# Two-layer hybrid backbone on one core: seams of layer 0 reordered, the even class's sums a step earlier, odd classes' stores on another queue

## The chip, the cores and the metric

One Trainium2 chip, one of its cores. The metric is the device time of one execution in microseconds; lower is better. The core has five engines with a queue of their own each: TensorE (PE, matmuls), VectorE (DVE), ScalarE (ACT), GpSimd (POOL) and SyncE (SP). Each runs its own instructions in order and waits on semaphores for the others'. Transfers are issued here by SP (`ld`) and by POOL (`ldr`), now and then by ACT (`lda`), and stand in the issuing engine's order.

## The reference

Two layers over 1024 latent tokens and 256 context tokens of width 1024, all float32. Cut to what matters here:

```python
def swiglu(u, w_gate, w_up, w_down):
    return (jax.nn.silu(u @ w_gate) * (u @ w_up)) @ w_down
def long_conv(u, filt, skip):
    uf = jnp.fft.rfft(u, n=2 * L, axis=1)
    ff = jnp.fft.rfft(filt, n=2 * L, axis=0)
    return jnp.fft.irfft(uf * ff[None], n=2 * L, axis=1)[:, :L] + u * skip
def hyena_mix(p, ...):
    x1, x2, v = jnp.split(short_conv(p, conv_w, conv_b), 3, axis=-1)
    filt = hyena_filters(L, w1, b1, freq, w2, b2, w3)
    v = x1 * long_conv(v, filt[:, 0], skip[0])
    return x2 * long_conv(v, filt[:, 1], skip[1])
def mixer_ab(u, ...):                       # layer 0
    p = u @ w_in
    return jnp.concatenate([fourier_mix(p[..., :512]), hyena_mix(p[..., 512:], ...)], axis=-1) @ w_out
# layer 1: neighbourhood attention, 16 heads, bias rpb by relative position; latents also see the context
for i in range(2):
    sh1, sc1, g1, sh2, sc2, g2 = split(silu(cond) @ ada_w[i] + ada_b[i], 6)   # cond: c or c_ctx
    h = h + g1 * mixer(rms_norm(h) * (1 + sc1) + sh1)
    h = h + g2 * swiglu(rms_norm(h) * (1 + sc2) + sh2, ...)
return rms_norm(h_lat, final_g)
```

The context tokens go through the same steps in layer 0; they have no output of their own in layer 1.

## The kernel before

Matmuls that need float32 accuracy take operands as a high and a low part: `split` casts the high part on ScalarE (`last_hi`, L350) and subtracts it on VectorE for the low part (`last_lo`, L352). Weights arrive in `ws` tiles (four buffers) and are split into `wh` and `wl` (two buffers each), so a pair can be split only when the pair two before it has been used. The other tiles come from pools with fixed counts: `s` (21 of 1024 columns, `S4`; 35 of 512, `S2`), `g` (4, `G`), `t` (6, `T`), `tk` (4, `TK`), and PSUM banks `ps` (6) and `pq` (2). A tile's name in the views is its pool's, without numbers.

The program is recorded from Python generators that yield after each step, so that stages can be woven: `next(g)` records one more step of a side stage. A scheduler then sets the order on each engine by a timeline of its own; `follow(x)` tells it to put what is recorded inside behind instruction x. After that each engine's order is fixed.

The stages by time in the profile: start and filter MLP to 56 us; the input projection (`in_proj`), woven with the long filters' taps (`filter_raw`) and spectra (`spectrum_l`, once per filter: about 145 to 207 and 262 to 317 us) and with the context's filters, to 430 us; the long convolutions forward and back to 635 us (`inverse_last` ends them); the output projection (`out_proj`) to 751.7 us; layer 0's FFN (`ffn`, then `down`) to about 1560 us; values, attention (about 1590 to 2190 us), its output projection and layer 1's FFN to the end.

The places that the change touches:

- `spectrum_l` multiplies a filter's taps with cosine and sine matrices (`ff_l`, loaded by POOL into `tk` tiles) in four classes, in the order 2, 3, 0, 1, each in two halves p with two operands k. Classes 0 and 2 are even, 1 and 3 odd. `operands()` makes an operand from sums of taps (`sums` for even classes, L958 to L970), and splits it; `ready` holds operands that are made ahead. TensorE's banks are copied out by ScalarE (L1043), the odd classes' by VectorE sums (L1051, L1053), and stored.
- `filter_raw` multiplies taps by windows `in_win_l` that SP loads; VectorE reads the banks at L822.
- `late_groups` loads the conditioning (`load_cond`), takes its silu (L556) and makes the last adaLN group by VectorE sums (L584). It is woven with `inverse_last` and `out_proj`.
- `out_proj` calls `after1` when a part of the columns is done. `rms_begin` adds up squares (`square`: ScalarE L609, VectorE L614) over the partitions by matmuls with a column of ones; `rms_end` spreads the result by two more.
- `ffn` first does the context's columns, 22 blocks of gate and up, with `second` (the norm of latent columns, `wino_second`) woven in.
- `down` ends in a loop of 22 blocks over the context's columns (L2230); `hook` weaves `after2` in: the norm of layer 1 for the columns done (`norm_block`: VectorE L656, ScalarE L658, VectorE L659).
- `attn_item` scores two chunks of one head; its position bias is loaded into two `g` tiles (c0 = 0) or a `bias` tile. The first 48 items are "cross": they use a `tk` tile for a transpose by DMA. The 16 items after them don't.

## Time and profile before

| | |
|---|---|
| runs | 2848.94 us median of 3 (2848.43 to 2850.37) |
| profiled execution | 2850.3 us, its span 2848.5 us |
| busy in the span | PE 97%, PEld (weight loads of TensorE) 81%, DVE 72%, ACT 46%, POOL 19% |
| DMA | 554.20 MB, mean 195 GB/s |
| granted TensorE clock | 0.99 of full speed, mean |

A row of the timeline gives start, duration, engine, line, operation, tile written <- tiles read, shape and count; in brackets stands how long the engine was idle before it, and what ended that. "PE ps L346 <- ACT s L1043: 3.6, 2, 3.2" reads: matmuls of line 346 waited 3.6 us in all, two times, at most 3.2 us, until ScalarE's L1043 was done. PEclk is the granted clock of TensorE as a share of full speed.

### The profile page before, as it was taken

How to read it: one execution, taken by the hardware profiler on the slowest of the kernel's cores; microseconds unless marked ns; L12 is line 12 of the kernel's file. 1: busy time of each engine (PE TensorE's matmuls, PEld its weight loads, DVE VectorE, ACT ScalarE, POOL GpSimd, SP SyncE). 2: the span in 40 equal slices, each digit the busy share in tenths (PEclk: the TensorE clock that was granted, in tenths of full speed). 3: DMA queues.
4: the chain of work that ended last, by engine and by line, in shares of the span. 5: the costliest groups of instructions: out<-in, count | busy, mean ns of one | idle time of the engine just before them, and what ended most of it. 6: DMA issues, size and time to landing. Idle time of an engine off the chain costs nothing. (4 is left out here: it accounts for less than half of the span.)

```text
span 2848.5 us, 43624 instructions
## 1 busy us (share of the span) xinstructions
PE 2762.6 (97%) x15610; PEld 2314.2 (81%) x15610; DVE 2044.6 (72%) x3531; ACT 1319.0 (46%) x2269; POOL 543.9 (19%) x880
## 2 busy tenths in 40 slices
PE   7999999999999999999999999999999999999998
PEld 4876778788898888888879888888887788888887
DVE  6767577867877888876777437778768977664556
ACT  5433336443554333333455337788755533333434
POOL 2210235331001221222020002333211122112000
PEclk9999999999999999999999999999999999999999
DMA  7356535665666656658884436877855366434763
GB/s 268 121 182 219 155 93 186 215 211 189 214 196 200 211 196 210 213 202 323 306 305 152 133 115 152 201 197 197 243 191 207 133 239 229 140 106 170 234 195 133
DMA packets 296886, 554.20 MB, mean 195 GB/s; under 512 B 81872, under 2 KB 128658, under 8 KB 296670
## 3 DMA queue, kind: packets, MB, share of 16 engines
q1 hardware_dynamic: 227966, 352.67, 39.4%
q0 software_dynamic: 61504, 185.65, 18.6%
q10 hardware_dynamic: 7200, 13.11, 1.4%
q8 instruction: 123, 2.02, 0.3%
q14 instruction: 93, 0.76, 0.1%
HBM read 405.01 MB, written 118.76 MB: 184 GB/s over the span
## 5 line engine op out<-in xcount | busy, mean ns | idle before, releaser
L1932 PE MATMUL ps<-s,s 128*128 128x512 f32 x2012 | 497.6, 391 | 3.5 <-DVE s L1823 1.9
L1932 PEld LDWEIGHTS ps<-s,s 128*128 128x128 f32 x2012 | 378.3, 188 | 84.0 <-DVE s L1823 3.2
L346 PE MATMUL ps<-s,wh 128*128 128x256 f32 (+1 forms) x1776 | 401.9, 331 | 10.8 <-ACT s L1043 3.2
L346 PEld LDWEIGHTS ps<-s,wh 128*128 128x128 f32 x1776 | 295.2, 190 | 46.4 <-ACT s L350 4.1
L346 PE MATMUL ps<-s,wl 128*128 128x256 f32 (+1 forms) x888 | 267.4, 329 | 1.7 <-DVE wl L352 1.6
L2109 PE MATMUL ps<-s,s 128*128 128x512 f32 (+1 forms) x1000 | 259.9, 383 | 3.3 <-DVE s L352 3.2
L350 ACT CAST s<-s 128x1024 fp32r<-128x1024 f32 (+2 forms) x192 | 172.6, 927 | 193.1 <-DMA s<-d 177.3
L346 PE MATMUL pq<-s,wh 128*128 128x512 f32 (+1 forms) x848 | 260.8, 389 | 0.4 <-ACT wh L350 0.3
L352 DVE TENSOR_TENSOR wl<-ws,wh 128x1024 fp32r<-128x1024 f32 (+1 forms) x141 | 168.3, 1195 | 119.8 <-ACT wh L350 114.2
L350 ACT CAST wh<-ws 128x1024 fp32r<-128x1024 f32 (+1 forms) x141 | 144.7, 1026 | 204.9 <-PE ps L346 85.0
L352 DVE TENSOR_TENSOR s<-s,s 128x1024 fp32r<-128x1024 f32 (+2 forms) x170 | 190.9, 1154 | 59.4 <-ACT s L350 59.1
L346 PE MATMUL ps<-s,s 128*128 128x65 f16 (+4 forms) x2736 | 226.2, 235 | 7.3 <-DVE st L2446 2.6
L350 ACT CAST s<-t 128x512 fp32r<-128x512 f32 (+2 forms) x238 | 133.9, 581 | 195.8 <-PE ps L1932 69.2
L2109 PEld LDWEIGHTS ps<-s,s 128*128 128x128 f32 x1000 | 184.5, 188 | 41.3 <-DVE s L352 5.0
L352 DVE TENSOR_TENSOR s<-t,s 128x512 fp32r<-128x512 f32 (+2 forms) x238 | 151.2, 651 | 72.6 <-ACT s L350 59.6
L1932 PE MATMUL ps<-s,wh 128*128 128x512 f32 x624 | 194.9, 390 | 0.0
L346 PEld LDWEIGHTS ps<-s,wl 128*128 128x128 f32 x888 | 165.6, 190 | 18.4 <-DVE wl L352 2.5
L337 POOL DMA_DIRECT2D d<-s x186 | 101.0, 544 | 375.5 <-DVE s L1739 92.5
L346 PEld LDWEIGHTS pq<-s,wh 128*128 128x128 f32 x848 | 151.1, 190 | 22.1 <-ACT wh L350 0.7
L346 PE MATMUL pq<-s,wl 128*128 128x512 f32 (+1 forms) x424 | 162.0, 382 | 0.6 <-DVE wl L352 0.6
L2109 PE MATMUL ps<-s 128*128 128x512 f32 (+1 forms) x500 | 150.9, 385 | 0.0
L346 PEld LDWEIGHTS ps<-s,s 128*128 128x128 f32 (+1 forms) x816 | 126.6, 192 | 21.8 <-ACT t L2448 2.7
(486 smaller groups left out, 5465.0 us busy)
## 6 DMA issues: line engine op xcount, KB each, us to landing
s<-d SPq DMA_DIRECT2D x282, 256.0 KB, 3.9
d<-s POOLq DMA_DIRECT2D x170, 256.0 KB, 3.7
s<-in_down SPq DMA_DIRECT2D x150, 256.0 KB, 4.2
s<-in_ada_w POOLq DMA_DIRECT2D x64, 512.0 KB, 4.9
ws<-in_up SPq DMA_DIRECT2D x44, 512.0 KB, 3.7
d<-g POOLq DMA_DIRECT2D x86, 256.0 KB, 3.0
ws<-in_gate SPq DMA_DIRECT2D x42, 512.0 KB, 4.8
d<-tk POOLq DMA_DIRECT2D x66, 256.0 KB, 4.0
```

The lines of the kernel that those rows point to most:

```text
L337: self.last_ldr = self.nc.gpsimd.dma_start(out, in_).ins
L346: self.last_mm = self.nc.tensor.matmul(o, l, r, start=st, stop=sp).ins
L350: self.last_hi = nc.scalar.copy(hi, src).ins
L352: self.last_lo = eng.tensor_tensor(lo, src, hi.bitcast(F32), SUB).ins
L1932: nc.tensor.matmul(ps, x[:, sl], y, start=first and j == 0 and x is wh and y is xh, stop=j == 3 and x is wl, skip_group_check=True)
L2109: m = nc.tensor.matmul(acc[j][:, c0:c1], x[:, sl], y[:, xs], start=first and k == 0, stop=last and k == 2, skip_group_check=True)
```

## The change

Five groups of edits, all in the order of work and in where tiles and transfers go. No matmul is added or taken away; two activation table loads are added.

1. `spectrum_l`: class 0's f0 and its first sums are made during class 3's second half, behind that half's operands, all in `s2` tiles; operands are made three ahead instead of four; the odd classes' 16 stores go by POOL instead of SP.
2. `late_groups`: the silus are recorded three steps later, behind the inverse's last high cast.
3. `ffn` for layer 0: the first gate block's weights are loaded and split during the output projection (`early`), and the norm's `rms_begin` and `rms_end` of columns 512 to 1023 are steps of `second`, behind the first and the second block, not ahead of the FFN; `second` starts at the first block instead of the third.
4. `after2` for the columns 512 to 1023: one norm block per step instead of two, each behind the low part made two norm blocks earlier.
5. `attn_item`: the bias of items that are not cross, with hd = 0 and c0 = 0, goes to `tk` tiles.

```diff
@@ late_groups
-        self.load_cond(wide=where == "s4")
+        self.load_cond(wide=where == "s4", act=False)
+        yield
+        yield
+        yield
+        with self.follow(self.inv_hi):
+            for t in self.cond:
+                for x in t:
+                    self.nc.scalar.activation(x, x, AF.Silu)
@@ spectrum_l, sums
-            t, u, x = self.T(), self.S2() if i else self.T(), self.T() if i else self.S2()
+            t, u, x = (self.T(), self.S2(), self.T()) if i else (self.S2(), self.S2(), self.S2())
@@ spectrum_l, operands
+            even0 = []
             for i in classes:
-                if i == 0:
-                    f0 = self.f0 = self.S2()
...
-                even = []
+                even = even0 if i == 0 else []
...
-                            if p == 0:
+                            if p == 0 and i:
                                 even.append(sums(i, k))
...
                         yield xh, xl, mt[k]
+                        if i == 3 and p:
+                            if k == 0:
+                                f0 = self.f0 = self.S2()
...
+                            even0.append(sums(0, k))
 
         ops = operands()
-        ready = [next(ops) for _ in range(4)]
+        ready = [next(ops) for _ in range(3)]
@@ spectrum_l, odd classes
-                        self.ld(self.frg[("l", o, 1, f)][eo], x)
+                        self.ldr(self.frg[("l", o, 1, f)][eo], x)
...
-                        self.ld(d[eo], t)
+                        self.ldr(d[eo], t)
@@ inverse_last
+        self.inv_hi = self.last_hi
@@ ffn
-                gh, gl = self.weights(a["gate"][l, fb], wide=wide)
+                gh, gl = early.pop() if fb == 0 else self.weights(a["gate"][l, fb], wide=wide)
...
-                if fb >= 2:
-                    with self.follow(last):
-                        next(second, None)
+                with self.follow(last):
+                    next(second, None)
@@ attn_item
-            bias = [self.G(F32, 384), self.G(F32, 384)]
+            new = self.G if cross or hd else self.TK
+            bias = [new(F32, 384), new(F32, 384)]
@@ run
             else:
                 drain(first)
-                rest.append(self.rms((1,))[0])
 
         def first_row():
-            yield from self.wino_first(h, 0, 3, rest.pop())
+            for k, _ in enumerate(self.wino_first(h, 0, 3, rest.pop())):
+                if k == 6:
+                    self.p3 = 1
+                    early.append(self.weights(a["gate"][0, 0], wide=3))
+                yield
@@ run, after2
+            los = []
             for b in range(KB):
...
-                self.norm_block({b: h3.ap(0, b, pc)}, b, pc, 1, 0, u1, r)
-                if b % 2:
+                with self.follow(los.pop() if los and pc == 1 else None):
+                    self.norm_block({b: h3.ap(0, b, pc)}, b, pc, 1, 0, u1, r)
+                los.append(self.last_lo)
+                if b % 2 or pc == 1:
                     yield
@@ run
-        self.ffn(0, uf, h3, hs0, (x for r in rest for x in self.wino_second(h, 0, 3, r)), after2, hd)
+        def second():
+            with self.follow(self.last_mm):
+                c = self.rms_begin(1)
+            yield
+            with self.follow(self.last_mm):
+                r = self.rms_end(1, c)
+            yield
+            yield from self.wino_second(h, 0, 3, r)
+
+        self.ffn(0, uf, h3, hs0, second(), after2, hd, early=early)
```

In the changed kernel later lines have higher numbers (L1043 becomes L1053, L656 and L659 become L663 and L666).

What it does to the order, at three places. ScalarE in the second filter's spectrum, from the copies of class 2 to those of class 3 (`s` <- `t` are casts of operands), before:

```order
L1043 COPY s_669_2474<-ps_2443 128x512
L1043 COPY s_672_2478<-ps_2444 128x512
L962 CAST s_681_2505<-t_2501 1x512
L350 CAST s_683_2512<-t_2500 128x512
L350 CAST s_688_2529<-t_2523 128x512
L1043 COPY s_692_2540<-ps_2490 128x512
L1043 COPY s_695_2543<-ps_2491 128x512
L1068 ACTIVATE s_698_2575<-ps_2278,c_287 128x256
```

And after:

```order
L1053 COPY s_666_2468<-ps_2437 128x512
L1053 COPY s_669_2472<-ps_2438 128x512
L969 CAST s_676_2495<-s_674_2491 1x512
L350 CAST s_679_2504<-t_2502 128x512
L350 CAST s_686_2525<-s_673_2490 128x512
L1053 COPY s_690_2536<-ps_2484 128x512
L1053 COPY s_693_2539<-ps_2485 128x512
L1078 ACTIVATE s_696_2571<-ps_2278,c_287 128x256
```

Two casts stand between the one-row cast and the copies in both, but they are of other operands: before, of class 0's first two (t_2500 and t_2523, the results of L965 and L970); after, of class 3's last and class 0's first. Class 0's second has moved behind the copies.

VectorE at the end of layer 0, from two low parts of down weights (`wl`) into the norm of columns 512 to 1023, before:

```order
L352 TENSOR_TENSOR wl_14519<-ws_14517,wh_14518 128x1024
L656 SCALAR_TENSOR_TENSOR t_14583<-s_3020_12687,c_99,t_14505 128x512
L656 SCALAR_TENSOR_TENSOR t_14587<-s_3021_12689,c_99,t_14505 128x512
L656 SCALAR_TENSOR_TENSOR t_14630<-s_3022_12691,c_99,t_14505 128x512
L656 SCALAR_TENSOR_TENSOR t_14634<-s_3023_12693,c_99,t_14505 128x512
L656 SCALAR_TENSOR_TENSOR t_14674<-s_3078_12968,c_99,t_14505 128x512
L659 SCALAR_TENSOR_TENSOR s_3328_14581<-t_14583,c_99,s_3328_14581 128x512
L352 TENSOR_TENSOR wl_14553<-ws_14551,wh_14552 128x1024
```

And after:

```order
L352 TENSOR_TENSOR wl_14519<-ws_14517,wh_14518 128x1024
L663 SCALAR_TENSOR_TENSOR t_14583<-s_3020_12687,c_99,t_14505 128x512
L666 SCALAR_TENSOR_TENSOR s_3328_14581<-t_14583,c_99,s_3328_14581 128x512
L352 TENSOR_TENSOR wl_14553<-ws_14551,wh_14552 128x1024
L663 SCALAR_TENSOR_TENSOR t_14624<-s_3021_12689,c_99,t_14505 128x512
L352 TENSOR_TENSOR wl_14596<-ws_14594,wh_14595 128x1024
L663 SCALAR_TENSOR_TENSOR t_14664<-s_3022_12691,c_99,t_14505 128x512
L666 SCALAR_TENSOR_TENSOR s_3329_14582<-t_14624,c_99,s_3329_14582 128x512
L666 SCALAR_TENSOR_TENSOR s_3341_14662<-t_14664,c_99,s_3341_14662 128x512
L352 TENSOR_TENSOR wl_14634<-s_3338_14632,wh_14633 128x1024
```

Between low parts stand two, one and three instructions of the norm, where the first gap held six.

SP in the attention, where the last bias tiles of pair 7 are loaded (s <- d are reloads of attention outputs for the output projection), before:

```order
L331 DMA s_4631_22056<-d_15886 128x512
L331 DMA s_4641_22126<-d_15887 128x512
L331 DMA g_22037<-in_bias 128x384
L331 DMA s_4642_22128<-d_15888 128x512
L331 DMA g_22038<-in_bias 128x384
L331 DMA bias_22343<-in_bias 128x2x384
L331 DMA g_22237<-in_bias 128x384
```

And after:

```order
L331 DMA tk_22037<-in_bias 128x384
L331 DMA t_21520<-d_15137 32x4x128 x4
L331 DMA tk_22038<-in_bias 128x384
L331 DMA bias_21948<-in_bias 128x2x384
L331 DMA bias_22131<-in_bias 128x2x384
L331 DMA s_4584_21804<-d_15877 128x512
L331 DMA t_21690<-d_15137 128x2x128
```

The two loads 22037 and 22038 stood behind the reloads and now stand ahead of the first of them (s_4584).

More of the change, by code (lines that the diff above doesn't have):

```diff
@@ L978, in operands @@
         def operands():
+            even0 = []
             for i in classes:
-                if i == 0:
-                    f0 = self.f0 = self.S2()
-                    V.tensor_copy(f0, fe)
-                    V.tensor_tensor(f0[0:1, :], fe[0:1, :], fo[0:1, :], ADD)
-                    V.scalar_tensor_tensor(f0[0:1, :], f0[0:1, :], 0.5, self.taps0[o][0:1, :], op0=MUL, op1=ADD)
-                even = []
+                even = even0 if i == 0 else []
                 for p in (0, 1):
@@ L1005, in operands @@
                         yield xh, xl, mt[k]
+                        if i == 3 and p:
+                            if k == 0:
+                                f0 = self.f0 = self.S2()
+                                V.tensor_copy(f0, fe)
+                                V.tensor_tensor(f0[0:1, :], fe[0:1, :], fo[0:1, :], ADD)
+                                V.scalar_tensor_tensor(f0[0:1, :], f0[0:1, :], 0.5, self.taps0[o][0:1, :], op0=MUL, op1=ADD)
+                            even0.append(sums(0, k))
         ops = operands()
-        ready = [next(ops) for _ in range(4)]
+        ready = [next(ops) for _ in range(3)]
         yield
@@ L1975, in wino_begin, with ffn @@
         return s
-    def ffn(self, l, u, h, hs, second, after, keep=None, begun={}):
+    def ffn(self, l, u, h, hs, second, after, keep=None, begun={}, early=()):
         nc, a = self.nc, self.a
@@ L2002, in ffn @@
         if u is not None:
+            last = None
             for fb in range(NFB):
                 wide = 3 if fb < NFB - 2 else 2
-                gh, gl = self.weights(a["gate"][l, fb], wide=wide)
+                gh, gl = early.pop() if fb == 0 else self.weights(a["gate"][l, fb], wide=wide)
                 uh, ul = self.weights(a["up"][l, fb], wide=wide)
@@ L2652, in spill @@
                     self.ldr(hs[b][:, pc * 512:pc * 512 + WID[pc]], h.ap(0, b, pc))
-        rest = []
+        rest, early = [], []
         def after1(pcs):
```

## The prediction

> **What bounds the kernel now.** I read the page's busy line first, then the waits of TensorE by cause, then stretches of one clock window each, then the order of events around every wait that lies where the diff works.
>
> ```profile
> span 2848.5 us, 43624 instructions
> PE 2762.6 (97%) x15610; PEld 2314.2 (81%) x15610; DVE 2044.6 (72%) x3531; ACT 1319.0 (46%) x2269; POOL 543.9 (19%) x880
> ```
>
> TensorE is busy for all but 2848.5 - 2762.6 = 85.9 us, and the diff adds or removes no matmul. It can win only idle time of TensorE, and the time in which TensorE runs at half clock. The waits by cause (us in total, times, longest):
>
> ```profile
> engine line waited for: us in total, times, longest us
> ...
> PE pq L346 <- DVE s L822: 3.7, 3, 1.7
> PE ps L346 <- ACT s L1043: 3.6, 2, 3.2
> ...
> PE ps L2230 <- DVE wl L352: 3.0, 2, 2.1
> PE ps L346 <- DVE st L2446: 2.6, 1, 2.6
> ...
> PE pq L346 <- DVE tk L614: 2.3, 1, 2.3
> ...
> PE ps L346 <- DVE wl L352: 1.6, 1, 1.6
> ```
>
> The longest of each of these six lies at a place that the diff touches. A wait costs more than itself where the clock falls. In stretches of 3.4 us (busy columns PE to POOL, then the granted clock, DMA share, GB/s):
>
> ```profile
> core 0: us, PE busy (x) PEld busy (x) DVE busy (x) ACT busy (x) POOL busy (x), PEclk, DMA share, GB/s
> ...
> 281.80:285.20 3.40, 0.24 (x2) 0.24 (x3) 3.27 (x6) 1.39 (x3) 0.00 (x0) 0.99 0.57 139
> 285.20:288.60 3.40, 3.40 (x18) 3.40 (x17) 2.67 (x5) 3.40 (x7) 0.00 (x0) 0.50 0.11 39
> ...
> 755.90:759.30 3.40, 3.40 (x19) 3.40 (x18) 2.23 (x4) 2.61 (x6) 0.00 (x0) 0.54 0.82 251
> 1534.10:1537.50 3.40, 1.61 (x15) 1.42 (x13) 3.40 (x5) 2.49 (x3) 0.00 (x0) 1.00 0.35 131
> 1537.50:1540.90 3.40, 3.09 (x14) 3.09 (x15) 3.40 (x6) 0.72 (x1) 0.00 (x0) 0.55 0.44 146
> ...
> 2070.00:2073.40 3.40, 3.02 (x33) 2.75 (x33) 2.18 (x7) 3.04 (x8) 0.00 (x0) 0.55 0.44 160
> ...
> 666.60:670.00 3.40, 2.80 (x14) 2.05 (x12) 3.40 (x12) 0.79 (x2) 0.87 (x2) 1.00 0.19 77
> 670.00:673.40 3.40, 2.37 (x14) 2.11 (x15) 3.40 (x9) 0.14 (x1) 0.55 (x2) 1.00 0.45 122
> ```
>
> After the waits of 3.21, 2.29, 2.10 and 2.57 us one stretch runs at about half clock: 3.4 us of work at half speed is 1.7 us lost. The 1.63 us at 669.4, split over two stretches (0.60 and 1.03 idle), costs no clock. So a stretch with some 1.8 us idle costs 1.7 us more, and where a smaller wait falls on the grid is luck.
>
> **The change part by part.** Terms are against the profiled execution (2850.3 us; its span is 2848.5).
>
> *Spectrum of the second long filter.* ScalarE casts operands in order, and its copies that empty TensorE's banks (L1043) stand among them:
>
> ```profile
> 279.54 0.62 ACT L350 CAST s<-t 128x512 fp32r<-128x512 f32 x1 [2.50 <-DVE t L965]
> 283.81 0.62 ACT L350 CAST s<-t 128x512 fp32r<-128x512 f32 x1 [3.65 <-DVE t L970]
> 284.33 1.06 ACT L1043 COPY s<-ps 128x512 f32<-128x512 f32 x2
> ...
> 284.96 0.64 PE L346 MATMUL ps<-s,wh 128*128 128x256 f32 x2 [3.21 <-ACT s L1043]
> ```
>
> Before, the cast at 283.81 waits for VectorE's L970 ahead of the two copies. With operands three ahead that cast stands behind them: the casts that remain in front need nothing later than L965's result, for which the row at 279.54 waited, so the copies end by about 281.2, before TensorE needs them at 281.75. The 3.21 us go, and the 1.7 of clock. What is late next: the last operand of class 3 now has its low part on VectorE behind the first sums, about 0.35 us too late. And the loads that GpSimd issues for class 1 get their buffers some 2.3 us before use:
>
> ```profile
> L337 POOL DMA_DIRECT2D tk<-in_ff_l x12: 527/528/597, 263.3 to 305.7; - x12
> ...
> DMA to landing us min/median/max: 2.5/4.4/7.0
> ```
>
> 4.4 - 2.3 = 2.1 us of wait, where today 1.0 us is lost (0.67 at 306.75, 0.34 at 309.08): +1.1, with ends 0 (landing in 2.5) and +3.7 (in 7.0). Waits: -3.2 + 0.35 + 1.1 = -1.8; clock -1.7. The even class's sums now lie in the s2 tiles instead of t; they are the same VectorE instructions, their f0 copy and first sums only pass behind one operand, so nothing is added to VectorE. The first filter's spectrum has the same reordering but waits under 1 us in all: 0, with ends -1.0 and +0.6.
>
> *Odd classes' stores by GpSimd.* SP loses 16 issues, POOL gains 16 of 0.53 us, 8.4 us on an engine that is busy 19%: nothing, while the loads behind them on POOL have slack, some 2 us for the tightest pair. On SP they stood ahead of the window loads:
>
> ```profile
> 211.51 0.69 DVE L822 TENSOR_TENSOR s<-pq,s 128x512 f32<-128x512 f32 x1 [3.02 <-DMA s<-in_win_l]
> ...
> 189.71 16.73 SPq L331 DMA_DIRECT2D d<-s  x7
> 206.49 0.99 SPq L331 DMA_DIRECT2D s<-in_win_l  x2
> ```
>
> SP was held 16.7 us until the odd class's sums existed. Without them the windows land before 208.5 and L822 starts 3 us sooner; TensorE's first wait for it, 1.67 us at 210.6, goes. But the next matmuls need a weight load whose buffer TensorE frees, and its landing sets their start, so most of the 1.3 and 1.4 us after it only merge to a longer wait that may cost clock. Between -1.7 (the first wait) and +1.0 I take -0.5.
>
> *Output projection's first weights.* VectorE has ten adaLN reductions (L584) between two low parts of weights, so the second comes late:
>
> ```profile
> 660.30:669.70 9.40, 6.91 (x19) 1.00 0.34 126
> ...
> 653.50 0.69 DVE L352 TENSOR_TENSOR s<-t,s 128x512 fp32r<-128x512 f32 x1 [3.98 <-ACT s L350]
> ```
>
> 6.9 of 9.4 us are L584 alone, and all of it is late because VectorE had waited 3.98 us for a cast that stood behind ScalarE's silus (L556), which wait for their loads. With the silus moved behind the inverse's last hi cast, four reductions pass ahead of the first low part and eight stay between: 2 x 0.67 less, and the inverse's low parts are done up to 4 us sooner. The 1.63 us go: -1.6, ends 0 and -1.9. The adaLN sums themselves are wanted some 40 us later, so their delay is hidden.
>
> *Seam to the FFN.* Before, the projection's last block is followed by a wait for the squares' sum and the eight column matmuls:
>
> ```profile
> 754.01 1.05 PE L346 MATMUL pq<-c,tk 128*128 128x1 f32 x8 [2.29 <-DVE tk L614]
> ...
> 760.89 1.28 ACT L2011 ACT_TABLE_LOAD   x1
> ```
>
> After, the first gate block, whose weights are split during the projection, runs in that wait. By the durations in these rows the new order goes: the first up block's low part ends 0.8 us late; rms_begin follows it, rms_end the next pair. The fourth gate block waits for its high part, which ScalarE has behind two casts that need VectorE's L1846 and L1853 after the row scale: 1.9 us. Two more table loads (1.28 us each) fall on ScalarE while TensorE works on blocks of 2.7 us, and are in these waits. So 2.29 becomes 2.7: +0.4; the clock's 1.7 is saved, as neither new wait fills a stretch by itself. Ends: -2.3 (no new wait) and +0.4.
>
> *End of layer 0.* VectorE does five and then seven of the norm's instructions ahead of low parts of weights that have only two buffers:
>
> ```profile
> 1527.45 3.40 DVE L656 SCALAR_TENSOR_TENSOR t<-s,c,t 128x512 f32<-128x512 f32 x5
> ...
> 1531.42 1.22 DVE L352 TENSOR_TENSOR wl<-ws,wh 128x1024 fp32r<-128x1024 f32 x1
> ...
> 1532.70 0.39 PE L2230 MATMUL ps<-s,wl 128*128 128x256 f32 x1 [0.91 <-DVE wl L352]
> 1537.81 0.57 PE L2230 MATMUL ps<-s,wl 128*128 128x256 f32 x1 [2.10 <-DVE wl L352]
> ```
>
> After, each block's norm follows the low part two back and at most three of its instructions (0.67 us apart) stand between low parts. TensorE spends 2.75 us on a block; 1.2 + 2.0 = 3.2 us is over that by 0.45 now and then, with 1.2 + 0.7 the next time: about 0.3 us of wait in all. -2.7, and the clock's -1.7; ends 0 and -4.7. The 1.59 us at 1492.65 belong to the first third's norm, which stays as it is.
>
> *Attention.* The late bias tiles of two heads:
>
> ```profile
> 2038.68 19.57 SPq L331 DMA_DIRECT2D s<-d  x20
> 2059.35 0.33 SPq L331 DMA_DIRECT2D g<-in_bias  x1
> ...
> 2061.59 0.33 SPq L331 DMA_DIRECT2D g<-in_bias  x1
> ...
> 2069.70 0.62 DVE L2446 CUSTOM_DVE_ANT_0 g<-ps,g,st 128x384 f32<-128x384 f32 x1 [3.21 <-DMA g<-in_bias]
> ```
>
> The g buffers come free late, so the two loads stand behind the twenty reloads of the outputs and take 10 us among them. With tk tiles, which no cross item uses any more, they stand ahead of those, at about 2023 to 2025. The 2.57 us go (-2.6), and the clock's -1.7. The waits of 0.94 and 0.97 us ten us earlier stem from a weight load, which stays. Ends 0 and -5.
>
> *Luck with the grid.* Waits of 1.6 to 2.1 us that remain or are new (1492, 2608, the class 1 load, the fourth gate block) meet one stretch about one time in three: four x 1.7 / 3 = +2.3, less the one hit now at 370 that may miss: +2.0.
>
> Waits: -1.8 - 0.5 - 1.6 + 0.4 - 2.7 - 2.6 = -8.8. Clock: 4 x -1.7 = -6.8, and +2.0. Sum -13.6: 2836.7 for an execution like the profiled one, which is 1.4 above the median of the three (2848.94), so 2835.3; I say 2835.5.
>
> **The rivals.** *The clock stays.* If the half-clock stretches came from something else than these waits, only the waits go: 2848.9 - 8.8 = 2840.1. Against it speaks that each follows its wait directly; the mean clock over the span says how much is at stake:
>
> ```profile
> core 0: 2848.5 us, clock 0.990
> ```
>
> 1% of 2848.5 is 28 us, some seventeen such stretches. The Trainium skill ("TensorE: Matmul & The Clock Gate", "HAM oscillation") gives as its abstract rule that only idle gaps of more than about 3.4 us lead to the slow clock; by it no wait here would cost clock and closing them would save none. The trace differs: it shows 0.55 after 2.10 us of idle. Chance 0.11.
>
> *The waits move on.* The work that made VectorE late is spread, not less: if the norm's blocks still delay every second low part by half a microsecond, the fourth gate block also takes its clock stretch, and the bias loads meet another late transfer, then the spectrum's and the projection's terms alone remain: -1.8 - 1.7 - 1.6 + 0.5 = -4.6, or 2844.3. For it speaks VectorE's load there (3.40 busy of 3.40 in two stretches above). Chance 0.15.
>
> *GpSimd's queue becomes the limit (slower).* A store on POOL waits for its sum, and the operand loads of classes 0 and 1 queue behind. If it holds them so that a pair starts when its predecessor is used, each of four pairs in two filters costs the whole landing and a stretch: 8 x (4.4 + 1.7) = 49 us, or 2884. It decides from 19.3 us in all (13.6 + 5.7), 2.4 us a pair. Against it: by the walk above the stores' sums are there near 293, and the load behind them, issued then, is wanted near 298, one landing later. The Trainium skill ("SBUF — State Buffer", "SBUF: two separate sides") warns that a transfer of the GpSimd queue stalls while VectorE runs a wide copy, since GpSimd can't write its descriptors, and advises the SP queue: a rule against this move. The trace shows issues of 527 to 597 ns while VectorE is 3.27 us busy of 3.40, so no such stall in issuing. Chance 0.06.
>
> **How the numbers follow.** The forecast has 0.68. Its own range: 2830 (no growth of the class 1 wait, no new wait at the gate, 1.1 + 2.7, and luck at the grid, 1.7) to 2841. The range goes from 2829.5 to 2844.5, which takes in the first two rivals and leaves out the third and both tails. A measurement of this kernel tells 0.2% (5.7 us) from no change: faster is below 2843.2. Forecast and first rival are faster, 0.79; the second is the same, 0.15; the third slower, 0.06.
>
> **What would show it.** Right: no TensorE wait for the spectrum's copies above 0.5 us; clock 1.00 in the stretches after 281, 1532 and 2067; SP's window loads ahead of 200; the first gate block straight behind the projection; no bias wait in attention. Wrong: the same waits under another name, above all a class 1 load wait over 3 us, a gate wait over 2.3 us, or low parts still late at the end of layer 0.

## The result and the profile after

The changed kernel takes 2837.61 us (median of 5, 2833.98 to 2842.97) against 2848.94: a ratio of 0.9953, interval 0.9937 to 0.997. Measured twice more, on two chips, it gave 0.9956 (0.994 to 0.9972) and 0.9955 (0.9943 to 0.9967). It is faster by about 12 us; 2835.5 was forecast.

The profiled execution of the changed kernel takes 2836.49 us. Its page, the core's clock, and TensorE's waits by cause (us in total, times, longest):

```profile
span 2834.7 us, 43636 instructions
PE 2756.6 (97%) x15610; PEld 2310.1 (81%) x15610; DVE 2042.6 (72%) x3531; ACT 1321.8 (47%) x2271; POOL 552.4 (19%) x896
```

```profile
core 0: 2834.7 us, clock 0.993
```

```profile
engine line waited for: us in total, times, longest us
...
PE ps L346 <- ACT wh L350: 3.8, 3, 2.7
...
PE ps L2241 <- DVE wl L352: 1.5, 2, 0.8
...
PE ps L346 <- DVE wl L352: 1.5, 2, 0.8
...
PE ps L2241 <- ACT wh L350: 1.4, 2, 1.1
...
PE pq L346 <- DMA tk<-in_ff_l: 1.2, 2, 0.6
...
PE ps L346 <- DMA tk<-in_ff_l: 1.0, 1, 1.0
...
PE pq L346 <- ACT s L1053: 0.8, 1, 0.8
```

(L2241 was L2230, L1053 was L1043.) Of the six waits that the prediction quoted, those for the bias (2.6) and the squares (2.3) are gone, and the one for the spectrum's copies is down from 3.2 to 0.8; L2230's for the low part fell from 3.0 to 1.5, but a new one, for the high part, has 1.4. The first line is partly new too: 2.73 us, which end at 214.75.

Stretches of 3.4 us (PE to POOL, granted clock, DMA share, GB/s) at the spectrum, the end of layer 0 and the attention:

```profile
core 0: us, PE busy (x) PEld busy (x) DVE busy (x) ACT busy (x) POOL busy (x), PEclk, DMA share, GB/s
...
276.80:280.20 3.40, 2.02 (x8) 1.10 (x7) 3.40 (x6) 2.35 (x5) 0.98 (x2) 1.00 1.06 355
280.20:283.60 3.40, 3.40 (x26) 3.20 (x25) 3.40 (x7) 1.23 (x3) 0.00 (x0) 1.00 0.10 27
...
1544.40:1547.80 3.40, 1.57 (x7) 1.37 (x8) 2.35 (x2) 1.97 (x2) 0.00 (x0) 0.87 0.49 190
1547.80:1551.20 3.40, 3.40 (x22) 3.40 (x21) 0.02 (x1) 0.16 (x1) 0.00 (x0) 0.63 0.55 154
...
2049.40:2052.80 3.40, 2.57 (x13) 1.88 (x12) 3.34 (x9) 2.26 (x8) 2.71 (x5) 1.00 1.06 290
2052.80:2056.20 3.40, 3.40 (x50) 3.34 (x49) 2.77 (x7) 3.40 (x9) 0.00 (x0) 1.00 1.03 341
```

The spectrum keeps 1.38 us of idle time in one stretch, and the clock stays at 1.00. At the end of layer 0 there are 1.83 us, and the clock falls. In the attention 0.83 us remain of the three waits there, and cost no clock.

To see where the time went, the trace is cut at the same matmuls, by their count, in every execution. Duration of each stage in us, the stages named by their times before; the last column is the mean of the three changed executions less before:

```
stage                       before   changed, three executions   mean difference
0-56    start                51.95    49.86   50.92   50.64        -1.5
205-222 filter windows       16.94    16.12   16.09   16.17        -0.8
262-318 second spectrum      55.95    51.12   53.32   51.08        -4.1
318-430 rest of in_proj     112.01   115.00  113.22  117.78        +3.3
635-751 out_proj            118.96   114.61  114.60  114.66        -4.3
751-800 seam to the FFN      46.05    47.34   48.34   47.42        +1.7
800-1480 FFN                680.02   680.03  683.06  680.02        +1.0
1500-1590 end of layer 0     90.08    90.99   89.00   88.33        -0.6
2040-2090 attention          50.04    43.10   43.68   43.10        -6.7
2190-2841 output, FFN       651.10   651.67  651.57  651.76        +0.6
all else                    963.72   963.46  967.06  964.43        +1.3
```

The three changed executions have spans of 2834.7, 2842.0 and 2836.6 us, 10.7 us less than before in the mean. TensorE's gaps over 0.1 us, from its first matmul on, sum to 66.7, 65.7 and 63.9 us against 74.1: 8.7 less in the mean. Half of the time at half clock, which is what it costs where TensorE works through it, is 16.1, 19.9 and 22.1 us against 25.6: 6.2 less. The rest, matmuls' own time, is longer by 4.8 (-10.1 from the first matmul to the last, less the two); 1.0 of it is the FFN's, and a slow stretch that holds idle time counts too dear.

The column "before" is one execution. The experiments below repeat it wherever they leave a stage's order as it was, and so tell how far one figure can be trusted. The second spectrum takes 54.3 to 56.0 us in five traces with the old order, and 51.1 to 53.3 in six with the new; the attention 47.7 to 50.1 in seven, and 43.1 to 43.7 in seven. These gains are clear of the spread. The end of layer 0 takes 88.1 to 91.5 in eight traces with the old order, and 88.3 to 91.0 in three with the new: nothing can be told there.

### The profile page after: what moved, and what is told of

Its sections match the earlier page's. It is cut to its first block, busy times and chain, and to the rows that moved or that the text cites. A ratio compares the mean times of both kernels' runs of the same rounds, so it can differ in the third digit from the quotient of the medians.

```text
span 2834.7 us, 43636 instructions
## 1 busy us (share of the span) xinstructions
PE 2756.6 (97%) x15610; PEld 2310.1 (81%) x15610; DVE 2042.6 (72%) x3531; ACT 1321.8 (47%) x2271; POOL 552.4 (19%) x896
## 5 line engine op out<-in xcount | busy, mean ns | idle before, releaser
L337 POOL DMA_DIRECT2D d<-s x202 | 110.0, 546 | 379.1 <-DVE s L1750 90.5
```

The source lines that it names most:

```text
L337: self.last_ldr = self.nc.gpsimd.dma_start(out, in_).ins
```

## The experiments

Each ratio is against runs of the kernel before on the same chip (its medians there 2851.7 to 2852.3 us).

**e1_sums: the spectra's sums alone**, without the stores' move.

```diff
-            t, u, x = self.T(), self.S2() if i else self.T(), self.T() if i else self.S2()
+            t, u, x = (self.T(), self.S2(), self.T()) if i else (self.S2(), self.S2(), self.S2())
...
-                            if p == 0:
+                            if p == 0 and i:
...
+                            even0.append(sums(0, k))
...
-        ready = [next(ops) for _ in range(4)]
+        ready = [next(ops) for _ in range(3)]
```

> The kernel before with the spectrum's reordering alone: class 0's sums during class 3, in s2 tiles, operands three ahead; the odd classes' stores stay on SP. Theory A (each part is worth the waits that it closes, and 1.7 us for each slow stretch): the copies' wait of 3.21 us at 281.7 and the slow stretch behind it go, so the stage from 262 to 318 us becomes 4 to 5 us shorter, as in the whole change (4.8), and the time about 2844.5. Rival B (the stage needs the stores on GpSimd too, since SP's queue holds loads that class 0 wants): under 2 us shorter, time about 2847. In both the window loads at 206 us stay late, so the waits at 210 to 218 us stay 4.3 us.

Measured: 262 to 318 takes 51.08 us, 4.9 less. But the time is 2855.2, ratio 1.0005 (0.9995 to 1.0016): the gain is real in its place and absent from the sum. The window loads stay late, as expected, yet the waits near them are 3.3 us in place of 4.3, one of them 2.4 long with a slow stretch behind it, so that 205 to 262 us gains nothing (57.2 against 56.9).

**e2_stores: the odd classes' stores alone.**

```diff
-                        self.ld(self.frg[("l", o, 1, f)][eo], x)
+                        self.ldr(self.frg[("l", o, 1, f)][eo], x)
...
-                        self.ld(d[eo], t)
+                        self.ldr(d[eo], t)
```

> The kernel before with the odd classes' 16 stores issued by GpSimd, nothing else. Theory A: the window loads are issued near 198 instead of 206 us and the stretch from 205 to 222 us gets 0 to 1 us shorter, since the weight behind it then sets the end; the copies' wait of 3.2 us in the second spectrum stays; time 2848 to 2849. Rival B (GpSimd's queue becomes the limit): the operand loads of classes 0 and 1 come late, class 1 waits for its tk tiles over 3 us in each filter, and the time rises by 4 us or more. Rival C: the 3 us that the whole change lost between 318 and 430 us come from these stores, whose tiles are freed later; then that stretch is about 3 us longer here.

Measured: 205 to 222 takes 16.15 us, 0.8 less, as in the changed kernel; 262 to 318 takes 55.34. TensorE's waits for the operand loads there grow from 1.1 to 2.4 us, but no store stands in GpSimd's queue just ahead of the loads it waits for, so rival B is out. Rival C may hold in part: 318 to 430 takes 114.6, 2.6 more, though e3, which leaves that order alone, takes as much. The time is 2856.44, ratio 1.0016 (1.0004 to 1.0028), a small loss.

**e10_spectrum: both spectrum edits**, to find where their gain goes.

> The kernel before with both edits of the spectra: sums a step earlier in small tiles with operands three ahead, and the odd classes' stores by GpSimd. Nothing else. Theory A (the two are worth what the profile of the changed kernel shows in their stages): 205 to 222 us takes 16.1 (0.8 less), the second spectrum's stage (262 to 318) 51 to 53 against 56, and the time is 4 to 5 us below before. Rival B (what the stage gains is given back: the class 1 loads wait behind the stores on GpSimd's queue, or 318 to 430 us grows by the 3 us seen in four profiles): the stage gains 3 to 5, 318 to 430 is 114 to 116 again, and the time is within 2 us of before, as with the sums alone.

Measured: 16.06 and 51.08 us in the two stages, 5.7 less together; 2851.94 us in all, ratio 1.0 (0.9989 to 1.001). Rival B was right that it is given back, and wrong on where: 318 to 430 takes 113.1, within the 112.0 to 114.6 of kernels whose order there is that of before. Most of it, 4.5 of 5.7 us, is lost at the start of layer 1, 1,900 us later. A TensorE row, and its stretches there:

```profile
2265.62 5.49 PE L1935 MATMUL pq<-s,s 128*128 128x512 f32 x12 [3.15 <-ACT g L1940]
```

```profile
core 0: us, PE busy (x) PEld busy (x) DVE busy (x) ACT busy (x) POOL busy (x), PEclk, DMA share, GB/s
...
2261.80:2265.20 3.40, 0.67 (x3) 0.20 (x2) 3.40 (x6) 0.22 (x1) 0.99 (x2) 0.95 0.95 308
2265.20:2268.60 3.40, 2.98 (x7) 2.40 (x8) 2.87 (x5) 0.37 (x1) 2.47 (x6) 0.50 0.87 296
```

The stage from 2235 to 2285 takes 49.9 us before, 48.8, 49.0 and 49.3 in the changed kernel, and 49.1 to 49.4 in e3, e4, e6 and e8_no_norm; it takes 54.0, 55.7 and 54.4 in e1, e2 and e10. Before and in the five kernels of the first kind the order of TensorE there (its matmuls from 80 to 90% of the trace, 1,561 rows) is the same to the row. In e1, e2 and e10, 72, 456 and 72 of these rows work on another tile than the same row before, although the edits lie in layer 0. So part of what an edit does comes from an order that it wasn't meant to touch.

**e4_bias: the bias in `tk` tiles alone.**

```diff
-            bias = [self.G(F32, 384), self.G(F32, 384)]
+            new = self.G if cross or hd else self.TK
+            bias = [new(F32, 384), new(F32, 384)]
```

> The kernel before with the attention's bias tiles alone (tk instead of g for the items that are not cross with hd = 0, c0 = 0). Theory A: the wait of 2.6 us for the bias at 2068 us goes, with it the slow stretch where that wait had one, and the waits of 0.9 and 1.0 us at 2057 to 2059 stay; from 2040 to 2090 us TensorE's idle time falls from 4.5 to about 2 us. Rival B (the whole change's stage has 0.8 us of idle time, so the waits at 2057 to 2059 had the same cause: loads that stand between the reloads on SP): idle time falls to about 0.8 us, as in the whole change, 4 us shorter and up to 7 where the clock was lost too. Rival C: the tk buffers hold up SP, and the stage stays at 48 us or more.

Measured: 2845.81 us, ratio 0.9974 (0.9965 to 0.9984). It is the one part with a clear gain of its own, 6 to 7 us. 2040 to 2090 takes 43.11 with 0.75 us idle, as rival B said. SP now takes the loads ahead of the reloads:

```profile
2022.51 0.36 SPq L331 DMA_DIRECT2D tk<-in_bias  x1
...
2033.38 10.71 SPq L331 DMA_DIRECT2D s<-d  x12
```

Of the two smaller waits ahead of it (0.94 and 0.97), e4 keeps these:

```profile
2058.18 0.59 PE L346 MATMUL ps<-s,s 128*128 128x384 f32 x2 [0.27 <-DVE s L2506]
2059.25 0.59 PE L346 MATMUL ps<-s,s 128*128 128x384 f32 x2 [0.48 <-DVE s L2468]
```

Part of them comes from a weight: ScalarE's cast of it waited 1.61 us for its load before, and waits 0.51 in e4 (the first row is of before, the second of e4):

```profile
2054.31 0.84 ACT L350 CAST wh<-ws 128x768 fp32r<-128x768 f32 x1 [1.61 <-DMA ws<-in_w_out]
```

```profile
2053.72 0.83 ACT L350 CAST wh<-ws 128x768 fp32r<-128x768 f32 x1 [0.51 <-DMA ws<-in_w_out]
```

GpSimd issues this weight's load at the same place in all traces, 4.5 to 4.9 us after the stage's first matmul. It takes 8.4 to 9.5 us to land in the seven traces without the edit and 7.8 to 8.2 in six of the seven with it; in e8_again it takes 9.1, and the wait of 0.97 is there again. So it tends to land earlier with the edit, and what makes it do so is not shown. The bias wait, too, has no size of its own: in the seven traces without the edit it ends 29.2 to 30.3 us after the stage's first matmul, and what the two waits ahead of it cost comes off it (it is 2.6 us in before, but 4.4 in e5 and e6, where the smaller waits add up to 0.8 and 0.7). All idle time of the stage together is 4.5 to 6.1 us without the edit, and 0.75 to 1.4 with it.

**e5_silu: the silus' move alone**, and **e6_seam: the early gate block and the norm inside `second` alone**, without the new norm order of `after2`.

```diff
-        self.load_cond(wide=where == "s4")
+        self.load_cond(wide=where == "s4", act=False)
...
+        with self.follow(self.inv_hi):
```

> The kernel before with the later silus alone. Theory A: the wait of 1.6 us for the low part at 669 us and most of the 3 us of smaller waits around it go; from 635 to 751 us the stage becomes 4.3 us shorter (119.0 to 114.6, as in the whole change), with idle time falling from 4.7 to 0.6 us. Rival B (the forecast's own figure): only the 1.6 us go.

> The kernel before with the FFN's seam alone (first gate block's weights early, rms_begin and rms_end as steps behind the first two blocks). Theory A: the wait of 2.29 us ahead of the FFN goes and waits of 2.0 us in all come behind it (0.7, 0.6 and 0.8 us), none of which costs a slow stretch; with the slow stretch that follows the wait in the kernel before, 751 minus 3 to 800 us becomes 1 to 3 us shorter. Rival B: new waits and their stretch take back all, and it is the same within 0.5 us.

Measured: the silus give 2848.02 us, ratio 0.9992 (0.998 to 1.0004), and 635 to 751 takes 117.01, 1.95 less; the wait for the second low part (1.6) is gone, and little else, as rival B said. The seam gives 2850.57, 0.9998 (0.9985 to 1.0011): 635 to 751 takes 118.10 and 751 to 800 takes 48.33, 2.3 more, for most of the 2.29 us wait, which stood in the first of these stages, was exchanged for three waits in the second:

```profile
PE ps L346 <- DVE wl L352: 1.5, 2, 0.8
PE ps L346 <- ACT wh L350: 0.6, 1, 0.6
```

These are e6's waits from 740 to 800 us; the changed kernel's are the same to the digit. The half-clock stretch is gone too. By the cut that the expectation names, 748 to 800 us, before takes 51.90 and e6 51.73: the same within 0.5, rival B's figure. The changed kernel takes 50.74, 51.73 and 50.82. The two executions with 51.73 ran the FFN's first matmuls at a slower pace (last section), which costs 1.0 here, so at one pace the seam is worth about 1.1 us. By waits and clock it should be 2.0; the matmuls themselves take 0.8 longer, and why stays open. The out_proj stage of the changed kernel (-4.3) thus holds both the silus' share and the seam's old wait, which stood just ahead of the cut.

**e3_norm: `after2`'s order alone**, and **e8_no_norm: the changed kernel without it.**

```diff
-                self.norm_block({b: h3.ap(0, b, pc)}, b, pc, 1, 0, u1, r)
-                if b % 2:
+                with self.follow(los.pop() if los and pc == 1 else None):
+                    self.norm_block({b: h3.ap(0, b, pc)}, b, pc, 1, 0, u1, r)
+                los.append(self.last_lo)
+                if b % 2 or pc == 1:
```

> The kernel before with after2's norm spread alone (one block a step, behind the low part two back). Theory A (the whole change won nothing at the end of layer 0 because the loads of every fifth down weight into s tiles stand on SP behind loads that wait for ws buffers): the waits for low parts (3.0 us) go, and two waits for the high part of a weight from an s tile come in their place, 1 to 2 us each, at the tenth and fifteenth block; from 1500 to 1590 us nothing is won (-1 to +1.5 us); time 2848 to 2850. Rival B (another part of the whole change disturbed it): the stretch becomes 3 us or more shorter and the time 2845 or less.

> The changed kernel with layer 1's first norm left as it was (two norm blocks per step, no follow). Theory A (the part is worth nothing in the changed kernel, because the loads into s tiles are late behind SP's held loads either way): 1500 to 1590 takes 90 to 91 us, as before, and the time is within 1 us of the changed kernel's. Rival B (the part is worth the 1.7 us that it had alone, a stretch at half clock): the stage is 90.1 and the changed kernel's own is 88.4 to 89; the time is about 2 us above the changed kernel's.

Measured: e3 takes 2851.3 us, ratio 0.9996 (0.9986 to 1.0006). Its end of layer 0 takes 88.38, 1.7 us less. The waits fall from 3.0 to 2.2 us and in part change their name; the half-clock stretch is missing:

```profile
PE ps L2230 <- DVE wl L352: 1.5, 2, 0.8
PE ps L2230 <- ACT wh L350: 0.7, 2, 0.4
```

That stretch is luck: in e2, e6 and e10, which keep the old order and its 3.0 us of waits there, it is missing as well. e8_no_norm takes 2837.97 us, ratio 0.9952 (0.9939 to 0.9966), beside the changed kernel's 2837.69: this part is worth nothing that can be measured here, as theory A said.

**e7_down_pool and e9_down_pool_again: why the norm's part brings so little.** In the changed kernel, SP's queue and ScalarE at the end of layer 0:

```profile
1508.03 15.63 SPq L331 DMA_DIRECT2D ws<-in_down  x5
1523.76 0.42 SPq L331 DMA_DIRECT2D s<-in_down  x1
1525.99 12.90 SPq L331 DMA_DIRECT2D ws<-in_down  x4
1538.94 0.46 SPq L331 DMA_DIRECT2D s<-in_down  x1
```

```profile
1528.35 1.05 ACT L350 CAST wh<-s 128x1024 fp32r<-128x1024 f32 x1 [0.96 <-DMA s<-in_down]
...
1544.38 1.04 ACT L350 CAST wh<-s 128x1024 fp32r<-128x1024 f32 x1 [1.73 <-PE ps L2241]
```

Every fifth down weight goes into an `s` tile. Its load needs no `ws` buffer, but stands behind five and four loads that do and hold SP for 15.6 and 12.9 us. The two casts of the high part start 0.1 us after these loads have landed (1528.25 and 1544.28), the second of them too, for which the row names TensorE. TensorE's four waits in this stage, 0.3 and 0.8, 1.1 and 0.8 us, are for these two high parts and for the low parts behind them. The experiment lets GpSimd issue these loads:

```diff
-                    self.ld(f.rearrange("p (r k) -> p r k", r=2), w[kb].rearrange("r p k -> p r k"))
+                    (self.ld if kb % 5 < 4 else self.ldr)(f.rearrange("p (r k) -> p r k", r=2), w[kb].rearrange("r p k -> p r k"))
```

> The changed kernel, and every fifth down weight of layer 0's last loop is loaded by GpSimd instead of SP. Theory A: these four loads are then issued before 1520 us, the waits at the tenth and fifteenth block (1.1 and 1.9 us) and the slow stretch behind the second go, 3 to 4.7 us, and the time is 2833 to 2834.5. Rival B (VectorE and ScalarE are the limit, the norm's three instructions between low parts): the waits move to the low parts, and the time stays at 2837.

> The changed kernel with the weight loads that go into s tiles (every fifth block of layer 0's last loop) issued by GpSimd instead of SP, a second time, now beside the changed kernel itself. Theory A (the norm's spread is worth what was forecast once these loads are out of SP's queue): its end of layer 0 (1500 to 1590) takes about 86.5 us against 89 to 91 of the changed kernel, idle at most 0.7 us, no half-clock stretch; the time is 3 to 4 us below the changed kernel's. Rival B (the loads on GpSimd only move the lateness, to the loads of the next stage or to the output stores): the stage is short again, but 1590 to 1700 gives it back and the time is within 1 us of the changed kernel's.

Measured: 1500 to 1590 takes 86.53 and 87.01 us, with 0.4 and 0.6 idle and no slow stretch; the cast follows its predecessor at once. In e9:

```profile
1507.11 0.71 POOL L337 DMA_DIRECT2D s<-in_down  x1 [0.33 <-issue]
```

```profile
1541.39 1.03 ACT L350 CAST wh<-s 128x1024 fp32r<-128x1024 f32 x1
```

So the cause is shown. Theory A's figure for the stage holds, and its figure for the time does not. The time is 2841.02 (ratio 0.9957, 0.9943 to 0.9972) and 2838.61 (0.9962, 0.9949 to 0.9974), no better than the changed kernel. Neither theory had the reason: again the start of layer 1 was ordered anew. 148 of the 1,561 rows of TensorE between 80 and 90% of the trace differ from the changed kernel's, and 2235 to 2285 takes 55.5 and 55.7 us. ScalarE's order there against the changed kernel's (+ is e7, e9):

```
-L1948 COPY tk_24086<-ps_23620 128x512
 L350 CAST s_5250_24127<-t_24124 128x512
 L350 CAST s_5252_24131<-t_24123 128x512
+L1948 COPY tk_24086<-ps_23620 128x512
```

In e9 a store then comes late (25.5 us after the first matmul of 2235 to 2285, 22.1 in the changed kernel), the copy into the store's tile waits for its landing, and TensorE for the copy; the changed kernel's wait at that place follows:

```profile
2241.78 0.54 POOL L337 DMA_DIRECT2D d<-g  x1 [7.88 <-DVE g L2037]
...
2247.28 0.59 ACT L1948 COPY g<-pq 128x512 f32<-128x512 f32 x1 [7.18 <-DMA d<-g]
...
2247.92 5.35 PE L1943 MATMUL pq<-s,s 128*128 128x512 f32 x12 [5.15 <-ACT g L1948]
```

```profile
2252.66 3.02 PE L1943 MATMUL pq<-s,s 128*128 128x512 f32 x12 [0.68 <-ACT g L1948]
```

A version with these loads on GpSimd and layer 1's old order would be some 3 us faster than the changed kernel; that is an estimate from the stages, and was not run.

**e8_again and e11_after: the changed kernel as it is**, beside the others.

> The changed kernel as it is, on the same chip as the three parts, to see what their sum leaves open and how far its stages differ from execution to execution. Theory A: the stages that the change touches repeat within 0.5 us plus 1.7 for each slow stretch that comes or goes; those it does not touch differ by as much as the stages of the other kernels do (up to 8 us at the start of layer 1); median against before 0.995 to 0.997. Rival B (luck made a good part of the result): 0.998 or above.

> The changed kernel, unchanged, as the measure of the other three on the same chip: 0.995 to 0.996 of before. In its profile the stage 1500 to 1590 between 89 and 91 us, 2040 to 2090 at 43, 635 to 751 at 114.6; 318 to 430 between 112 and 115 if that stage's spread is of the execution and not of the change.

Measured: 2839.62 and 2837.69 us, the ratios above. Their stages are in the table: the gains at 205, 635 and 2040 repeat within 0.6 us, 262 to 318 within 2.2, while 318 to 430 goes from 113.2 to 117.8 and the FFN takes 680 or 683. Two figures expected for e11 were missed: 1500 to 1590 takes 88.33, below 89, and 318 to 430 is 2.8 above the 115 that was to show a spread of the execution. Its waits there are no longer than in the other two (7.3 us against 8.0 and 8.1), but five windows of 3.4 us run at half clock, where the others have two and one. In e8_again the second spectrum is 2.2 us longer for the same kind of reason: an operand load was issued as soon as TensorE freed its buffer, landed 6.2 us later (5.1 in the first execution), and a slow stretch followed the wait:

```profile
282.43 0.97 PE L346 MATMUL pq<-s,tk 128*128 128x512 f32 x3 [1.93 <-DMA tk<-in_ff_l]
```

## Why the prediction came out right

The sum held, 2837.61 against 2835.5, and its two halves nearly so: waits -8.7 against -8.8, clock -6.2 against -4.8. A third part, +4.8 of matmuls' own time, the sum did not have. Its terms held less well, and that the misses cancelled is luck. Of the signs it named, SP's window loads stand ahead of 200, the first gate block stands straight behind the projection, and attention has no bias wait; but the copies' wait is 0.8 and not below 0.5, and the late low parts at the end of layer 0 (1.5 us) were named as a sign of being wrong.

- **Spectrum, -1.8 - 1.7 forecast, -4.1 measured** (mean; -4.8 and -4.9 in two of three). All of TensorE's waits in the stage before:

```profile
PE ps L346 <- ACT s L1043: 3.2, 1, 3.2
PE ps L346 <- DVE s L1053: 1.4, 1, 1.4
PE pq L346 <- DMA tk<-in_ff_l: 0.8, 2, 0.4
PE pq L346 <- ACT s L1043: 0.7, 1, 0.7
PE ps L346 <- DMA tk<-in_ff_l: 0.3, 1, 0.3
```

  The 3.2 went whole; the 0.8 for copies that is left stood here as 0.7. The loads of `in_ff_l`, which were to cost +1.1 more, cost +0.5 (0.6 and 1.0 against 0.8 and 0.3). The 1.4 for VectorE's L1053 went as well, which the sum did not have. The clock's 1.7 is less sure: in three of the six traces with this order (e8_again, e7, e8_no_norm) a slow stretch follows the loads' waits, and in e5 and e6, with the old order and waits of 3.4 and 2.3 us, there is none. With all these traces the gain is 3.2 in the mean, against the 3.5 forecast.
- **Filter windows, -0.5 forecast, -0.8 measured.** The windows land early, as said, and the waits merge into one longer wait that costs a slow stretch:

```profile
196.29 5.37 SPq L331 DMA_DIRECT2D s<-in_win_l  x5
210.05 0.33 SPq L331 DMA_DIRECT2D ws<-in_w_in  x1
```

```profile
214.75 1.72 PE L346 MATMUL ps<-s,wh 128*128 128x256 f32 x6 [2.73 <-ACT wh L350]
```

- **Output projection and seam, -1.6 + 0.4 - 1.7 = -2.9 forecast, -4.3 + 1.7 = -2.6 measured.** The wait of 1.63 went (e5: -1.95). The seam's 2.29 became 2.1 in three pieces (1.5 in two, and 0.6) instead of 2.7 in two, and cost no clock; of the 0.2 and the 1.7 that this makes, some 1.1 us arrived.
- **End of layer 0, -2.7 - 1.7 forecast, -0.6 measured: the step that failed.** The estimate of "about 0.3 us of wait in all" counted VectorE's instructions between low parts and took the weights as there. Once VectorE was early, the next thing late was the weight in the `s` tile, from SP's queue; e7 and e9 show it by taking that away (-3.6 and -3.1 against before). The -0.6 itself is inside the spread. The idle time fell from 3.0 to 1.8 to 2.9 instead of 0.3.
- **Attention, -2.6 - 1.7 forecast, -6.7 measured.** The right mechanism, too small. "The waits of 0.94 and 0.97 us ten us earlier stem from a weight load, which stays" took them for a cost apart from the bias. The weight's load came earlier (e4), they shrank from 1.91 to 0.83, and the slow stretch at 2060 went with them. And the wait of 2.57 was not the whole price of the late bias: without the edit every trace loses some 4.5 us or more in the waits together, since the bias wait grows where the other two shrink. Over all traces the stage gains 6.2 us in the mean.
- **Rest of the input projection, nothing forecast, +3.3 measured.** Of this 1.0 and 2.6 appear in e4 and e3, whose order there is that of before, so much of it is a spread between executions. The rest goes with the order that comes with GpSimd's stores. In all eight traces that have it the two waits for L822 (0.66 and 0.78) are replaced by one of 1.40 for a cast:

```profile
321.65 0.50 PE L346 MATMUL ps<-g,s 128*128 128x512 f32 x1 [1.40 <-ACT g L350]
```

  and the stage's waits are 7.3 to 8.3 us, against 6.7 to 7.4 in the five with the old order. Its time is 114.6 in the mean against 112.9, so some 1.8 us is a cost of the change that the sum put at nothing.
- **The start, -1.5**, and the luck with the grid of +2.0. The start takes 51.0 to 53.1 us in e3, e4 and e6, which leave its order as it was, and 49.9 to 54.4 in the changed kernel's executions, e7 to e10: it is a spread, and nothing to forecast. No run measures the +2.0 by itself; it is part of the -6.2 of the clock.

Of the rivals, *the clock stays* falls: the slow stretches at 285, 756 and 2070 went with their waits, and in all traces slow stretches follow idle time as the last section counts it. By the rule of the Trainium skill ("TensorE: Matmul & The Clock Gate", "HAM oscillation") that only gaps of more than some 3.4 us cost clock, none would have been there to lose; the count below contradicts it. *The waits move on* held at the end of layer 0 alone. *GpSimd's queue becomes the limit* is refuted by e2. The evidence that the prediction gave against it was none, for in the stretch that it quotes, 281.8 to 285.2, GpSimd issues nothing (POOL 0.00). In the changed kernel the twelve operand loads of the second spectrum are issued in the same time as before and land as soon (before: 527/528/597 and 2.5/4.4/7.0):

```profile
L337 POOL DMA_DIRECT2D tk<-in_ff_l x12: 527/530/541, 260.2 to 299.4; - x12
...
DMA to landing us min/median/max: 2.5/4.0/6.0
```

From 285 to 291.8 VectorE is busy 3.40 of 3.40 us in each stretch, and GpSimd's six issues there take 0.53 to 0.56 us each. The Trainium skill ("SBUF — State Buffer", "SBUF: two separate sides") warns of a stall of that queue while VectorE runs such operations as a float32 copy from SBUF to SBUF. VectorE runs sums and products there, and none of the few such copies of this trace falls together with an issue of GpSimd, so the warning is not tested here.

## What to carry to other kernels

Before crediting the removal of a wait, name what is late next, down to the queue in which its load stands: here a load that needed no buffer stood behind loads that did. Where a scheduler sets the order, compare the whole program's order, not only the edited stage: an edit 1,900 us earlier cost 4 to 6 us in a stage that it never names. And judge small edits by their own stage in several executions before trusting the total.

## What the runs showed of the hardware that was not expected

- **How much idle time costs the clock.** In the 14 traces the slow stretches begin on a grid of 3.413 us. Counting grid windows at full clock after the first 60 us: with 1.9 us or more of TensorE idle in the window, 63 of 64 were followed by half clock; with 1.4 to 1.9 us, 41 of 93; with less, 20 of 11,055. The idle time may be in pieces, and a wait that falls across two windows counts in each for its part: e5's wait of 3.39 us, 1.80 and 1.60 in its two windows, cost no clock. The prediction's "some 1.8 us" lies in the middle band, and its stretches were not cut on the grid: of the 1.63 us at 669.4, 1.47 fall in one window.
- **Matmuls of one column count as idle.** Of the 20 exceptions 19 hold such matmuls, which the profile shows as busy; this row of before is followed by half clock at 148.6, after 0.55 us of idle in its window:

```profile
144.97 1.84 PE L346 MATMUL ps<-c,s 128*128 128x1 f32 x16
```

  With their time counted as idle the bands become 80 of 81, 43 of 115, and 1 of 11,016. The seam's slow stretch at 756 is one of them: its window holds 1.22 us of the wait and eight such matmuls.
- **One pace of matmuls in two values.** From the start of the FFN (about 775 us) to about 875, at clock 1.00, the changed kernel's first execution runs 90 to 91 matmuls in 10 us, e7's 87 to 88:

```profile
800.00:810.00 10.00, 10.00 (x91) 10.00 (x90) 7.22 (x10) 5.29 (x8) 1.08 (x2) 1.00 0.74 228
```

```profile
800.00:810.00 10.00, 10.00 (x88) 10.00 (x87) 7.43 (x9) 4.80 (x8) 0.91 (x2) 1.00 0.70 225
```

  The FFN then takes 683.06 instead of 680.02 us from 800 us on, and 1.0 to 1.5 us more before that (in e6, e7, e8_again and e10). The same program shows both (e8_again and e11_after), so it is no effect of the change; what decides it stays open.
